# Seven-product MLP: input tiles in pairs, the first chunk as a pipeline over pairs, GpSimd out of the cross output stage, six weight blocks ahead

## The chip, the core and the metric

The kernel runs on one core of one Trainium2 chip. The metric is the device time of one execution in microseconds (us), as a median over runs. TensorE is called PE here, VectorE DVE, ScalarE ACT, GpSimd POOL and SyncE SP, as the profile calls them.

## The reference

A decoder trunk of two layers, 512 tokens, model width 1024, all in float32. In each layer

```
h = h + W_out [ MLA(n) | DiffAttn(n) | MoBA(n) ],  n = RMSNorm(h)
h = h + CrossAttn(RMSNorm(h), RMSNorm(mem))
h = h + W2 relu(W1 RMSNorm(h))^2
```

and the trunk ends with a final RMSNorm. The change touches two places of a layer: the output projection of the cross attention (a 1024 x 1024 matrix, `w_co`), and the MLP behind it (`w1` 1024 x 4096, `w2` 4096 x 1024).

## The kernel before

**Number format.** Every operand of a matmul is held as two halves, a rounded part ("hi") and the rest ("lo"), side by side in one tile. A product is three matmuls: hi with hi, hi with lo, lo with hi (`mm3`). So every weight block that arrives by DMA costs one ACT cast (hi, L157 or L266) and one subtraction on DVE or POOL (lo, L162 or L267), and so does every activation tile (`split`, L140 and L142).

**The cross output stage** (`output` with `halves`, L1058). For m = 0 to 7 in this order, 24 matmuls of 128x512 (8 input tiles, 3 matmuls each) give 128 rows of the projection; DVE adds them to the residual tile `h[m]` (L1056); `half_input` (L1072) then makes the inputs of the MLP from it. For m < 4 that is the block called 11 and the difference t1. For m >= 4 it is 21, 22, and, with the scaled tile y that was kept from m - 4, the combinations t2, t3 and t4. Squares of h are summed over m (L409 on ACT, L412 on POOL, the last on DVE) for the norm. The w_co blocks are halved on DVE and POOL in turn (L162).

**The MLP** works in four chunks c of 1024 hidden columns, each in four pairs g = 0 to 3, called a to d below (two blocks of 128 hidden columns each). A pair is computed with seven products instead of eight, Strassen's way: product n takes one combination of the four quarter blocks of w1 (11, 12, 21, 22, or the sums s1 to s4) and one combination of the inputs:

```
FACTORS = {1: ("11", "11"), 2: ("12", "21"), 3: ("s4", "22"), 4: ("22", "t4"), 5: ("s1", "t1"), 6: ("s2", "t2"), 7: ("s3", "t3")}
```

A product is 4 input tiles x 3 matmuls = 12 matmuls of 128x256. "1a" is product 1 of pair a of the first chunk. Products 1 and 5 need only the inputs of m < 4; 2, 3, 4, 6 and 7 need those of m >= 4 too. `combination` (L242) fetches the quarter blocks, forms a sum on DVE (L263), casts on ACT (L266) and subtracts on DVE (L267); L1291, L1293, L1295 and L1300 (ACT) and L1288 and L1296 (DVE) collect the products from PSUM, and `evict` (L1308 to L1311) applies the squared ReLU. The products of a chunk are followed by the "down" blocks with w2, which run beside the products of the next chunk.

**What sets the order.** `planned` lists all weight blocks in the order of use, `mlp_order` those of the MLP. `weights` keeps `look` blocks ahead of the one in use: 2 until the MLP begins, then `mlp_look` = 6. In the MLP `vector_all` keeps the subtractions on DVE. All weight loads are issued by SP, in order. Tiles rotate through a few places each: `raw` has 4, `w` 5, `tmp` 11; of PSUM banks `mm` has 3 and `s` has 3. The order within each engine's queue is then fixed when the program is built; each engine works its queue in that order.

Of the kernel before, what the change touches and what calls it, by code (L numbers as in the profile page):

```python
# [17 lines left out]
KT = 8  # L18
# [83 lines left out]
class Trunk:  # L102
# [62 lines left out]
    def planned(self):  # L165

        a = self.a

        def halves(t):
            return [t[:, :S], t[:, S:]]  # L170

        for l in range(L):
            names = {"kv": [0], "cq": [1, 2], "d0": [3, 4], "d1": [5, 6]}
            names.update({n: [7 + 3 * j, 8 + 3 * j, 9 + 3 * j] for j, n in enumerate(("d2", "o0", "o1"))})
            for n in self.fill_order.split():
                for j in names.get(n, ()):
                    yield from halves(a["w_in"][l, j])
                if n == "tok":
                    for k in range(KT):
                        yield a["w_v"][l, k]  # L180
                if n[0] == "m" and n != "mem":
                    yield from (a["w_mla"][l, int(n[1]), :, :4 * P], a["w_mla"][l, int(n[1]), :, 4 * P:])
                if n == "cross":
                    for m in range(KT):
                        yield from halves(a["w_ck"][l, m])
                    for j in range(2 * KT):
                        yield a["w_cv"][l, j]
            for w in (a["w_out"][l], a["w_cq"][l], a["w_co"][l]):
                for m in range(KT):
                    yield from halves(w[m])  # L190
            for kind, c, m in self.mlp_order(l):
                if kind == "down":
                    yield from halves(a["w2"][l, c, m])
                else:
                    yield l, c, m, self.FACTORS[kind][0]
# [14 lines left out]
        return w  # L210

    FACTORS = {1: ("11", "11"), 2: ("12", "21"), 3: ("s4", "22"), 4: ("22", "t4"), 5: ("s1", "t1"), 6: ("s2", "t2"),
               7: ("s3", "t3")}

    @staticmethod
    def mlp_order(l):


        late = []
        for g in range(KT // 2):
            parts = [4, 3] if late else [None, None]
            for n, then in zip((1, 5, 2, 6, 7), (None, None, None, *parts)):
                yield n, 0, g
                if then:
                    yield then, 0, late[0]
            late = [g]
        for n in (4, 3):
            yield n, 0, late[0]  # L230
        for c in range(4):
            for g in range(KT // 2):
                if c < 3:
                    for n in (1, 5, 6, 2, 7):
                        yield n, c + 1, g
                yield "down", c, 2 * g
                if c < 3:
                    for n in (4, 3):
                        yield n, c + 1, g
                yield "down", c, 2 * g + 1  # L240

    def combination(self, l, c, g, name):  # L242

        nc = self.nc
        got = self.quads.setdefault((l, c, g), {})

        def block(n):
            if n not in got:
                src = self.a["w1"][l, c * KT + 2 * g + int(n[0]) - 1]
                t = self.sb.tile([P, S], F32, tag=tags[n], name=self.name("raw"), bufs=self.bufs[tags[n]])  # L250
                at = (int(n[1]) - 1) * S
                nc.sync.dma_start(t, src[:, at:at + S])
                got[n] = t
            return got[n]

        tags = {"11": "raw", "21": "raw", "12": "tmp", "22": "tmp"}
        sums = {"s1": ("21", "22", ALU.add), "s2": ("s1", "11", ALU.subtract), "s3": ("11", "21", ALU.subtract),
                "s4": ("12", "s2", ALU.subtract)}
        if name in sums:
            x, y, op = sums[name]  # L260
            x, y = (got[n] if n in sums else block(n) for n in (x, y))
            got[name] = self.tmp()
            nc.vector.tensor_tensor(got[name], x, y, op)  # L263
        raw = got[name] if name in sums else block(name)
        w = self.pair("w" if name in ("12", "22", "s4") else "B")
        nc.scalar.copy(w[:, 0, :], raw)  # L266
        nc.vector.tensor_tensor(w[:, 1, :], raw, w[:, 0, :].bitcast(F32), ALU.subtract)  # L267
        return w
# [789 lines left out]
    def output(self, w, outs, gain, order=range(KT), halves=None):  # L1058

        self.sum_squares_start()  # L1060
        hn = []
        for m in range(KT):
            ps = self.proj(w[m], lambda k: (outs[k][:, 0, :], outs[k][:, 1, :]), S, order)
            self.add_to_h(m, ps)
            if halves is None:
                hn.append(self.norm_input(m, gain))
            else:
                self.half_input(m, gain, halves)
        self.hn = hn
        self.hnorm = self.norm(self.sq, NQ, 2)  # L1070

    def half_input(self, k, gain, parts):  # L1072


        nc = self.nc
        n = S // 2
        j = k % 4
        y = self.tmp()
        nc.scalar.activation(y, self.h[k], AF.Copy, scale=gain[:, k:k + 1])  # L1079
        p = self.pair("A")  # L1080
        if k < KT // 2:
            self.split(p[:, 0, :n], p[:, 1, :n], y[:, :n])
            nc.vector.tensor_tensor(y[:, :n], y[:, n:], y[:, :n], ALU.subtract)
            self.split(p[:, 0, n:], p[:, 1, n:], y[:, :n])
            parts["11"].append(p[:, :, :n])
            parts["t1"].append(p[:, :, n:])

            parts["y"].append(y)
        else:
            self.split(p[:, 0, :], p[:, 1, :], y)  # L1090
            parts["21"].append(p[:, :, :n])
            parts["22"].append(p[:, :, n:])
            if j == 0:
                a, b, c = self.prob_tile(), self.prob_tile(), self.pair("B")
                parts["t23"] = [t[:, :, i * S:(i + 1) * S] for t in (a, b) for i in range(2)]
                parts["room"] = a[:, :, 2 * S:], b[:, :, 2 * S:], c[:, :, :n], c[:, :, n:]
            two, one = parts["t23"][j], parts["room"][j]
            t = self.tmp()
            nc.vector.tensor_tensor(t.rearrange("p (a c) -> p a c", c=n),
                                    y[:, n:].unsqueeze(1).to_broadcast([P, 2, n]),  # L1100
                                    parts["y"][j].rearrange("p (a c) -> p a c", c=n), ALU.subtract)
            nc.vector.tensor_tensor(y[:, :n], y[:, :n], t[:, :n], ALU.subtract)  # L1102
            self.split(two[:, 0, :], two[:, 1, :], t)
            self.split(one[:, 0, :], one[:, 1, :], y[:, :n])
            parts["t2"].append(two[:, :, :n])
            parts["t3"].append(two[:, :, n:])
            parts["t4"].append(one)
        self.sum_squares_add(self.h[k], k == KT - 1)

    def memory_norm(self, ticks, step):  # L1110

# [278 lines left out]
    def run(self):  # L1390
# [25 lines left out]
        g = self.gains  # L1416
# [11 lines left out]
        for l in range(L):  # L1428
            gs = slice(l * KT, (l + 1) * KT)
            self.vector_full = True  # L1430
            outs = self.mixer(l)
            self.vector_full = False
            self.output(self.a["w_out"][l], outs, g["g_cross"][:, gs], (3, 0, 4, 1, 5, 2, 6, 7))
            outs = self.cross(l)
            parts = {n: [] for n in ("11", "21", "22", "t1", "t2", "t3", "t4", "y")}
            self.output(self.a["w_co"][l], outs, g["g_mlp"][:, gs], halves=parts)
            self.vector_all, self.look = True, self.mlp_look
            self.mlp(l, g["g_attn"][:, (l + 1) * KT:(l + 2) * KT] if l + 1 < L else None, parts)
            self.vector_all, self.look = False, 2

# [100 lines left out]
```

## Time and profile before

| | |
|---|---|
| median of 3 runs | 1551.61 us (1550.52 to 1551.83) |
| the profiled execution | 1549.21 us, span 1547.4 us |
| PE busy | 1487.4 us, 96% of the span, 8648 matmuls |
| DVE busy | 1081.7 us, 70% |
| ACT busy | 854.6 us, 55% |
| POOL busy | 414.6 us, 27% |
| cross output stage and first MLP chunk, first layer | 389 to 492 us |
| the same, second layer | 1144 to 1246 us |

The two stages of the change come once in each layer. The span is that of the profiled execution, and its time is 2.40 us below the median of the unprofiled runs. Shares of the whole span say little here, since the stages have different limits; the rows below are of the two stages.

### The profile page before, as it was taken

To read this page: it belongs to the slowest core of one execution; us is meant where nothing else is said; L and a number is where in the kernel's file an instruction comes from. 1 tells how busy PE (TensorE), PEld (TensorE's weight loads), DVE (VectorE), ACT (ScalarE), POOL (GpSimd) and SP (SyncE) were. 2 spreads that over 40 slices of the span, in tenths; PEclk is the share of its full clock that TensorE was granted. 3 is DMA by queue.
4 is the path that set the end of the run, shared out by engine and by line. 5 is a ranking of instruction groups with operands and counts; after the bars stand their busy time and mean duration, and the time that the engine had idled before them with its cause. 6 is when DMAs were issued, how large, how long until landed. Compare 5 with 4: busy or idle time off the path is not lost.

```text
span 1547.4 us, 24601 instructions
## 1 busy us (share of the span) xinstructions
PE 1487.4 (96%) x8648; PEld 1299.8 (84%) x8648; DVE 1081.7 (70%) x2391; ACT 854.6 (55%) x1884; POOL 414.6 (27%) x336
## 2 busy tenths in 40 slices
PE   7799999999989999999998999999998999999997
PEld 5678797888879989988887878888887998998886
DVE  7688888535689667675437898883378986677653
ACT  5566778535456445454436667764355654454441
POOL 5645365342310000000136445644512000000001
PEclk9999999999999999999999999999999999999998
DMA  4444454221223332332324535423302333323321
GB/s 141 123 112 127 124 151 122 80 97 49 75 78 115 96 103 92 106 110 89 96 75 107 148 100 151 132 83 102 101 29 69 103 110 102 102 96 110 109 96 55
DMA packets 90141, 157.25 MB, mean 102 GB/s; under 512 B 12065, under 2 KB 17057, under 8 KB 90017
## 3 DMA queue, kind: packets, MB, share of 16 engines
q1 hardware_dynamic: 89728, 155.63, 32.6%
q8 instruction: 68, 1.11, 0.3%
q14 instruction: 57, 0.46, 0.1%
q10 hardware_dynamic: 288, 0.05, 0.0%
HBM read 136.24 MB, written 2.10 MB: 89 GB/s over the span
## 4 chain that ended last, share of the span: by engine, by line
PE 76%; DVE 14%; ACT 4%; issue 3%; POOL 1%; DMA 1%; SPq 0%; POOLq 0%; DVEq 0%; ACTq 0%
PE mm L279 60%; PE s L279 12%; PE t L282 3%; DVE tmp L635 2%; DVE B L142 1%; DVE tmp L700 1%; ACT tmp L637 1%; DVE pt L660 1%; DVE A L142 1%; PE t L279 1%; POOL w L162 1%; ACT tmp L1079 1%; DVE small L977 1%; DVE tmp L1102 1%; ACT B L140 1%
## 5 line engine op out<-in xcount | busy, mean ns | idle before, releaser
L279 PE MATMUL mm<-B,w 128*128 128x512 f32 (+1 forms) x2490 | 571.3, 386 | 3.9 <-DVE B L145 2.2
L279 PEld LDWEIGHTS mm<-B,w 128*128 128x128 f32 x2490 | 451.8, 188 | 98.5 <-DVE tmp L881 3.0
L279 PE MATMUL mm<-A,w 128*128 128x512 f32 (+1 forms) x1920 | 389.5, 353 | 16.8 <-ACT A L144 5.8
L279 PEld LDWEIGHTS mm<-A,w 128*128 128x128 f32 x1920 | 313.3, 192 | 63.7 <-DVE A L145 5.9
L157 ACT CAST w<-raw 128x512 fp32r<-128x512 f32 (+1 forms) x372 | 225.1, 607 | 256.2 <-PE mm L279 187.2
L162 POOL TENSOR_TENSOR w<-raw,w 128x512 fp32r<-128x512 f32 (+2 forms) x199 | 255.3, 1292 | 275.0 <-ACT w L157 248.6
L412 POOL TENSOR_TENSOR tmp<-tmp,tmp 128x512 f32<-128x512 f32 (+1 forms) x37 | 46.5, 1257 | 693.5 <-ACT tmp L409 672.6
L162 DVE TENSOR_TENSOR w<-raw,w 128x512 fp32r<-128x512 f32 x173 | 122.1, 706 | 27.0 <-ACT w L157 26.8
L637 ACT ACTIVATE tmp<-tmp,small 128x384 f32<-128x384 f32 (+3 forms) x176 | 99.1, 563 | 71.1 <-DVE small L635 65.8
L1056 DVE TENSOR_TENSOR h<-mm,h 128x512 f32<-128x512 f32 x92 | 63.2, 687 | 69.4 <-PE mm L279 69.3
L279 PE MATMUL mm<-pt,B 128*128 128x256 f32 x768 | 102.8, 283 | 0.3 <-ACT tmp L1293 0.3
L140 ACT CAST B<-tmp 128x512 fp32r<-128x512 f32 (+2 forms) x156 | 91.6, 591 | 19.3 <-DVE tmp L779 4.4
L266 ACT CAST B<-tmp 128x512 fp32r<-128x512 f32 x96 | 59.6, 621 | 69.3 <-DVE tmp L263 69.0
L279 PEld LDWEIGHTS mm<-pt,B 128*128 128x128 f32 x768 | 96.5, 191 | 0.8 <-ACT tmp L1293 0.5
L263 DVE TENSOR_TENSOR tmp<-raw,raw 128x512 f32<-128x512 f32 x64 | 44.0, 687 | 65.0 <-DMA raw<-w 65.0
L142 DVE TENSOR_TENSOR B<-tmp,B 128x512 fp32r<-128x512 f32 (+1 forms) x110 | 81.4, 740 | 11.1 <-ACT B L140 8.3
L282 PE MATMUL t<-ident,tmp 128*128 128x128 f32 (+1 forms) x444 | 73.9, 273 | 8.5 <-DVE tmp L825 4.6
L142 POOL TENSOR_TENSOR B<-tmp,B 128x512 fp32r<-128x512 f32 (+1 forms) x46 | 62.5, 1366 | 44.5 <-ACT B L140 39.3
L282 PEld LDWEIGHTS t<-ident,tmp 128*128 128x128 f32 (+1 forms) x444 | 54.3, 140 | 22.9 <-DVE tmp L825 5.4
L660 DVE TENSOR_TENSOR pt<-t,pt 128x256 fp32r<-128x256 f32 (+1 forms) x192 | 66.9, 370 | 7.0 <-ACT pt L657 6.0
L279 PE MATMUL s<-pt,B 128*128 128x512 f32 (+3 forms) x352 | 71.0, 345 | 0.0
L657 ACT CAST pt<-t 128x256 fp32r<-128x256 f32 (+1 forms) x192 | 58.0, 333 | 16.3 <-PE t L282 15.6
(194 smaller groups left out, 2137.3 us busy)
## 6 DMA issues: line engine op xcount, KB each, us to landing
raw<-w SPq DMA_DIRECT2D x256, 256.0 KB, 2.8
raw<-w_in SPq DMA_DIRECT2D x64, 256.0 KB, 3.2
st<-B SPq DMA_DIRECT2D x144, 64.0 KB, 2.0
raw<-w_ck SPq DMA_DIRECT2D x32, 256.0 KB, 3.0
raw<-w_cv SPq DMA_DIRECT2D x32, 256.0 KB, 2.6
raw<-w_out SPq DMA_DIRECT2D x32, 256.0 KB, 2.8
raw<-w_cq SPq DMA_DIRECT2D x32, 256.0 KB, 2.6
raw<-w_co SPq DMA_DIRECT2D x32, 256.0 KB, 2.6
```

Of the source, the lines that this page charges most:

```text
L140: nc.scalar.copy(hi, x)
L142: eng.tensor_tensor(lo, x, hi.bitcast(F32), ALU.subtract)
L157: self.nc.scalar.copy(w[:, 0, :], raw)
L162: eng.tensor_tensor(w[:, 1, :], raw, w[:, 0, :].bitcast(F32), ALU.subtract)
L266: nc.scalar.copy(w[:, 0, :], raw)
L279: self.in_order(self.nc.tensor.matmul(out, lhs, rhs, start=start, stop=stop, skip_group_check=open), hold)
L282: self.in_order(self.nc.tensor.transpose(out, x, self.ident))
L412: eng.tensor_tensor(s[:, :n], s[:, :n], self.sq[:, :n], ALU.add)
L637: nc.scalar.activation(t[:, :n], t[:, :n], AF.Exp, bias=st[:, 0:1], scale=-1.0, accum_out=st[:, 1:2])
L657: nc.scalar.copy(hi, src)
L660: nc.vector.tensor_tensor(lo, src, hi.bitcast(F32), ALU.subtract)
L1056: nc.vector.tensor_tensor(self.h[m], ps, self.h[m], ALU.add)
```

## The change

Five edits, made for both layers:

1. The cross output stage goes through m in the order 0, 4, 1, 5, 2, 6, 3, 7 (`BY_PAIRS`), in the plan of the weights and in the loop.
2. `vector_all` is set before that stage, not after it: POOL no longer halves w_co blocks there, and the squares are summed on DVE (`sum_squares_add(..., True)`).
3. `look` becomes 6 at the seventh block of the stage (m = 3), not at the start of the MLP.
4. The first chunk's products follow a written list that mixes the pairs, 1a 5a 1b 5b first; the last two (4d, 3d) go in behind the first products of the second chunk.
5. The block "12" of the first chunk takes a `raw` place instead of a `tmp` one.

```diff
--- before.py
+++ after.py
@@ -185,9 +185,9 @@
                         yield from halves(a["w_ck"][l, m])
                     for j in range(2 * KT):
                         yield a["w_cv"][l, j]
-            for w in (a["w_out"][l], a["w_cq"][l], a["w_co"][l]):
-                for m in range(KT):
-                    yield from halves(w[m])
+            for n in ("w_out", "w_cq", "w_co"):
+                for m in range(KT) if n != "w_co" else self.BY_PAIRS:
+                    yield from halves(a[n][l, m])
             for kind, c, m in self.mlp_order(l):
                 if kind == "down":
                     yield from halves(a["w2"][l, c, m])
@@ -210,6 +210,9 @@
         return w
 
 
+    BY_PAIRS = 0, 4, 1, 5, 2, 6, 3, 7
+
+
 
     FACTORS = {1: ("11", "11"), 2: ("12", "21"), 3: ("s4", "22"), 4: ("22", "t4"), 5: ("s1", "t1"), 6: ("s2", "t2"),
                7: ("s3", "t3")}
@@ -218,21 +221,16 @@
     def mlp_order(l):
 
 
-        late = []
-        for g in range(KT // 2):
-            parts = [4, 3] if late else [None, None]
-            for n, then in zip((1, 5, 2, 6, 7), (None, None, None, *parts)):
-                yield n, 0, g
-                if then:
-                    yield then, 0, late[0]
-            late = [g]
-        for n in (4, 3):
-            yield n, 0, late[0]
+        for step in "1a 5a 1b 5b 2a 6a 2b 7a 6b 4a 3a 7b 1c 4b 5c 3b 2c 6c 1d 7c 5d 4c 2d 6d 3c 7d".split():
+            yield int(step[0]), 0, "abcd".index(step[1])
+        late = [(4, 0, 3), (3, 0, 3)]
         for c in range(4):
             for g in range(KT // 2):
                 if c < 3:
                     for n in (1, 5, 6, 2, 7):
                         yield n, c + 1, g
+                        if late:
+                            yield late.pop(0)
                 yield "down", c, 2 * g
                 if c < 3:
                     for n in (4, 3):
@@ -253,7 +251,7 @@
                 got[n] = t
             return got[n]
 
-        tags = {"11": "raw", "21": "raw", "12": "tmp", "22": "tmp"}
+        tags = {"11": "raw", "21": "raw", "12": "tmp" if c else "raw", "22": "tmp"}
         sums = {"s1": ("21", "22", ALU.add), "s2": ("s1", "11", ALU.subtract), "s3": ("11", "21", ALU.subtract),
                 "s4": ("12", "s2", ALU.subtract)}
         if name in sums:
@@ -1059,7 +1057,9 @@
 
         self.sum_squares_start()
         hn = []
-        for m in range(KT):
+        for i, m in enumerate(range(KT) if halves is None else self.BY_PAIRS):
+            if halves is not None and i == 6:
+                self.look = self.mlp_look
             ps = self.proj(w[m], lambda k: (outs[k][:, 0, :], outs[k][:, 1, :]), S, order)
             self.add_to_h(m, ps)
             if halves is None:
@@ -1105,7 +1105,7 @@
             parts["t2"].append(two[:, :, :n])
             parts["t3"].append(two[:, :, n:])
             parts["t4"].append(one)
-        self.sum_squares_add(self.h[k], k == KT - 1)
+        self.sum_squares_add(self.h[k], True)
 
     def memory_norm(self, ticks, step):
 
@@ -1433,8 +1433,8 @@
             self.output(self.a["w_out"][l], outs, g["g_cross"][:, gs], (3, 0, 4, 1, 5, 2, 6, 7))
             outs = self.cross(l)
             parts = {n: [] for n in ("11", "21", "22", "t1", "t2", "t3", "t4", "y")}
+            self.vector_all = True
             self.output(self.a["w_co"][l], outs, g["g_mlp"][:, gs], halves=parts)
-            self.vector_all, self.look = True, self.mlp_look
             self.mlp(l, g["g_attn"][:, (l + 1) * KT:(l + 2) * KT] if l + 1 < L else None, parts)
             self.vector_all, self.look = False, 2
```

What this does to the queues is shown at three places, in the first layer. The second layer's queues change in the same way.

PE at the start of the MLP. `mm_1131` is the bank of the last w_co block; A tiles are 11 and t1 (1075, 1083, 1091, 1099) or 21 and 22 (the others), pt tiles t2 and t3, B and w the weights. Before, the end of 1a, then 5a, 2a, the start of 1b, 6a:

```order
L279 MATMUL mm_1144_5059<-A_1099_4837,B_1133_5005 128x256 x3
L279 MATMUL s_1157_5102<-A_1075_4697,B_1137_5026 128x256 x3
L279 MATMUL s_1157_5102<-A_1083_4743,B_1137_5026 128x256 x3
L279 MATMUL s_1157_5102<-A_1091_4790,B_1137_5026 128x256 x3
L279 MATMUL s_1157_5102<-A_1099_4837,B_1137_5026 128x256 x3
L279 MATMUL mm_1160_5120<-A_1107_4884,w_1146_5062 128x256 x3
L279 MATMUL mm_1160_5120<-A_1119_4938,w_1146_5062 128x256 x3
L279 MATMUL mm_1160_5120<-A_1128_4989,w_1146_5062 128x256 x3
L279 MATMUL mm_1160_5120<-A_1139_5044,w_1146_5062 128x256 x3
L279 MATMUL mm_1173_5190<-A_1075_4697,B_1152_5077 128x256 x3
L279 MATMUL mm_1173_5190<-A_1083_4743,B_1152_5077 128x256 x2
L279 MATMUL mm_1144_5059<-pt_1108_4887,B_1148_5067 128x256 x6
```

Now, the end of 5a, then 1b, 5b, the column sums of the squares, 6a (A_1141 is the input of m = 3, the last of the four 11 and t1 tiles):

```order
L277 MATMUL s_1157_5102<-A_1141_5021,B_1133_4977 128x256 x3
L277 MATMUL mm_1162_5122<-A_1075_4697,B_1135_4982 128x256 x3
L277 MATMUL mm_1162_5122<-A_1095_4797,B_1135_4982 128x256 x3
L277 MATMUL mm_1162_5122<-A_1112_4895,B_1135_4982 128x256 x3
L277 MATMUL mm_1162_5122<-A_1141_5021,B_1135_4982 128x256 x3
L277 MATMUL s_1165_5141<-A_1075_4697,B_1139_5003 128x256 x3
L277 MATMUL s_1165_5141<-A_1095_4797,B_1139_5003 128x256 x3
L277 MATMUL s_1165_5141<-A_1112_4895,B_1139_5003 128x256 x3
L277 MATMUL s_1165_5141<-A_1141_5021,B_1139_5003 128x256 x3
L277 MATMUL t_1167_5157<-ones2_93,tmp_1151_5078 128x2 x4
L277 MATMUL mm_1154_5083<-pt_1084_4746,B_1147_5050 128x256 x6
L277 MATMUL mm_1154_5083<-pt_1085_4747,B_1147_5050 128x256 x6
```

Four products that need only the tiles of m < 4 now stand behind the last w_co block, where two stood; 2a has moved behind 6a.

DVE around the eviction of the last w_co block (`h7`). L1099, L1102 and L142 are `half_input`, L263 and L267 the sums and the lo halves of w1 blocks. Before:

```order
L267 TENSOR_TENSOR B_1133_5005<-raw_1132_5003,B_1133_5005 128x512
L263 TENSOR_TENSOR tmp_1136_5024<-raw_1134_5020,raw_1135_5022 128x512
L1056 TENSOR_TENSOR h7_84<-mm_1131_5002,h7_84 128x512
L267 TENSOR_TENSOR B_1137_5026<-tmp_1136_5024,B_1137_5026 128x512
L1099 TENSOR_TENSOR tmp_1140_5047<-tmp_1138_5042,tmp_1098_4835 128x512
L263 TENSOR_TENSOR tmp_1147_5065<-tmp_1136_5024,raw_1132_5003 128x512
L142 TENSOR_TENSOR A_1139_5044<-tmp_1138_5042,A_1139_5044 128x512
L142 TENSOR_TENSOR pt_1109_4888<-tmp_1140_5047,pt_1109_4888 128x512
L1102 TENSOR_TENSOR tmp_1138_5042<-tmp_1138_5042,tmp_1140_5047 128x256
L412 TENSOR_TENSOR tmp_1141_5054<-tmp_1141_5054,tmp_1130_4999 128x512
L142 TENSOR_TENSOR B_1110_4889<-tmp_1138_5042,B_1110_4889 128x256
L267 TENSOR_TENSOR B_1148_5067<-tmp_1147_5065,B_1148_5067 128x512
```

Now, up to the same eviction, behind the sum s1a (L261 and L265 are L263 and L267 of before, L410 is L412, L1054 is L1056):

```order
L265 TENSOR_TENSOR B_1129_4968<-raw_1128_4966,B_1129_4968 128x512
L1054 TENSOR_TENSOR h3_76<-mm_1123_4955,h3_76 128x512
L265 TENSOR_TENSOR B_1133_4977<-tmp_1132_4975,B_1133_4977 128x512
L265 TENSOR_TENSOR B_1135_4982<-raw_1134_4980,B_1135_4982 128x512
L261 TENSOR_TENSOR tmp_1138_5001<-raw_1136_4997,raw_1137_4999 128x512
L261 TENSOR_TENSOR tmp_1146_5048<-tmp_1132_4975,raw_1128_4966 128x512
L410 TENSOR_TENSOR tmp_1142_5027<-tmp_1142_5027,tmp_1122_4952 128x512
L265 TENSOR_TENSOR B_1139_5003<-tmp_1138_5001,B_1139_5003 128x512
L142 TENSOR_TENSOR A_1141_5021<-tmp_1140_5019,A_1141_5021 128x256
L265 TENSOR_TENSOR B_1147_5050<-tmp_1146_5048,B_1147_5050 128x512
L1083 TENSOR_TENSOR tmp_1140_5019<-tmp_1140_5019 128x256
L1054 TENSOR_TENSOR h7_84<-mm_1143_5030,h7_84 128x512
```

Eight sums and lo halves of w1 blocks, enough for 1a, 5a, 1b, 5b and 6a, have moved ahead of the eviction of `h7`, where two stood.

SP, the loads of the first chunk. `raw` in a name is that of the fetched block, whatever place it takes. Before, in order 11a, 21a, 11b, 21b, 22a, 12a, 22b, 11c:

```order
L252 DMA raw_1132_5003<-w1 128x512
L252 DMA raw_1134_5020<-w1 128x512
L252 DMA raw_1151_5075<-w1 128x512
L252 DMA raw_1153_5080<-w1 128x512
L252 DMA raw_1135_5022<-w1 128x512
L252 DMA raw_1145_5060<-w1 128x512
L252 DMA raw_1154_5082<-w1 128x512
L252 DMA raw_1177_5210<-w1 128x512
```

Now 11a, 21a, 11b, 21b, 22a, 22b, 12a, 12b:

```order
L250 DMA raw_1128_4966<-w1 128x512
L250 DMA raw_1130_4971<-w1 128x512
L250 DMA raw_1134_4980<-w1 128x512
L250 DMA raw_1136_4997<-w1 128x512
L250 DMA raw_1131_4973<-w1 128x512
L250 DMA raw_1137_4999<-w1 128x512
L250 DMA raw_1144_5031<-w1 128x512
L250 DMA raw_1155_5084<-w1 128x512
```

12a now takes the place of 11a and 12b that of 21a among the four `raw` places, so both loads wait until DVE has formed s3a from 11a and 21a, and everything behind them on SP waits too.

## Rows read from the trace of the kernel before

**Rows 1.** Windows, first layer: PE, PEld, DVE, ACT, POOL busy (count), PEclk, DMA, GB/s.

```profile
394.40:433.00 38.60, 38.60 (x169) 31.38 (x168) 29.85 (x37) 21.46 (x40) 14.21 (x11) 1.00 0.25 83
433.00:448.00 15.00, 9.97 (x54) 8.97 (x54) 13.35 (x23) 8.02 (x15) 0.53 (x1) 0.77 0.25 87
448.00:491.80 43.80, 42.63 (x358) 42.07 (x357) 39.99 (x74) 30.42 (x63) 1.40 (x1) 1.00 0.28 91
491.80:740.00 248.20, 248.20 (x1546) 222.80 (x1545) 167.69 (x284) 119.24 (x224) 0.00 (x0) 1.00 0.32 102
```

**Rows 2.** The same windows of the second layer, behind its cross output stage.

```profile
1188.60:1203.60 15.00, 10.88 (x60) 10.20 (x59) 13.33 (x23) 8.37 (x17) 0.51 (x1) 0.77 0.25 85
1203.60:1246.20 42.60, 41.77 (x352) 41.44 (x352) 39.97 (x74) 30.14 (x63) 1.40 (x1) 1.00 0.29 93
```

**Rows 3.** Timeline of PE, first layer: start, length, matmuls, idle before and its releaser.

```profile
395.60 37.47 PE L279 MATMUL mm<-B,w 128*128 128x512 f32 x163
...
434.82 0.51 PE L279 MATMUL mm<-A,B 128*128 128x256 f32 x2 [1.75 <-ACT B L266]
...
441.39 0.80 PE L279 MATMUL mm<-A,w 128*128 128x256 f32 x2 [2.43 <-ACT w L266]
...
448.01 0.95 PE L279 MATMUL t<-ones,tmp 128*128 128x2 f32 x8
448.82 0.96 PE L279 MATMUL mm<-A,B 128*128 128x256 f32 x6
...
453.53 0.62 PE L282 MATMUL t<-ident,rcol 128*128 128x128 f32 x4 [0.84 <-DVE rcol L347]
453.91 1.68 PE L279 MATMUL mm<-A,w 128*128 128x256 f32 x12
...
459.65 1.58 PE L279 MATMUL s<-A,w 128*128 128x256 f32 x12
...
473.81 1.60 PE L279 MATMUL mm<-A,w 128*128 128x256 f32 x12
...
491.77 5.66 PE L279 MATMUL mm<-B,w 128*128 128x512 f32 x24
```

**Rows 4.** Timeline of PE, second layer: last w_co matmuls, first down block.

```profile
1186.65 1.99 PE L279 MATMUL mm<-B,w 128*128 128x512 f32 x8
...
1246.17 5.20 PE L279 MATMUL mm<-B,w 128*128 128x512 f32 x22
```

**Rows 5.** DVE groups by form, 394 to 433 us: count, busy us, mean ns, idle before.

```profile
L142 DVE TENSOR_TENSOR A<-tmp,A 128x256 fp32r<-128x256 f32 x8 | 7.2, 900 | 5.8 <-ACT A L140 5.8
L1083 DVE TENSOR_TENSOR tmp<-tmp 128x256 f32<-128x256 f32 x4 | 4.6, 1139 | 0.2
L1102 DVE TENSOR_TENSOR tmp<-tmp,tmp 128x256 f32<-128x256 f32 x3 | 4.4, 1473 | 0.1
```

**Rows 6.** Timeline of DVE, three instructions back to back.

```profile
445.03 0.69 DVE L263 TENSOR_TENSOR tmp<-raw,raw 128x512 f32<-128x512 f32 x1
445.63 0.42 DVE L1288 TENSOR_TENSOR tmp<-mm,tmp 128x256 f32<-128x256 f32 x1
445.96 0.68 DVE L263 TENSOR_TENSOR tmp<-tmp,raw 128x512 f32<-128x512 f32 x1
```

**Rows 7.** Timeline of DVE and POOL at one moment of the cross output stage.

```profile
420.75 1.30 POOL L412 TENSOR_TENSOR tmp<-tmp,tmp 128x512 f32<-128x512 f32 x1 [3.87 <-ACT tmp L409]
420.83 1.50 DVE L1102 TENSOR_TENSOR tmp<-tmp,tmp 128x256 f32<-128x256 f32 x1
```

**Rows 8.** Timeline of ACT and POOL: half input, cast, and the power for the norm.

```profile
436.80 0.72 ACT L1079 ACTIVATE tmp<-h,gains 128x512 f32<-128x512 f32 x1
437.55 0.62 ACT L140 CAST A<-tmp 128x512 fp32r<-128x512 f32 x1
...
449.24 1.40 POOL L341 TENSOR_TENSOR small<-small,mhalf 128x4 f32<-128x4 f32 x1 [15.71 <-DVE small L375]
```

**Rows 9.** Loads of line 252, 405 to 500 us, from issue to landing.

```profile
DMA to landing us min/median/max: 2.5/3.0/4.8
```

## The prediction, as it was made before the changed kernel ran

> **What bounds the kernel now.** I read the windows by stage first, then PE's timeline in the stretch that they point to, then DVE's groups there. In the cross output stage PE is busy 38.60 of 38.60 us, and in the later chunks of the MLP 248.20 of 248.20, both at granted clock 1.00: nothing that DVE, ACT, POOL or a load does there costs anything as long as PE is fed. Between them PE is busy only 9.97 of 15.00 us at a mean clock of 0.77 (a mix of the two levels, 2.4 and 1.2 GHz), then 42.63 of 43.80, while DVE is busy 13.35 of 15.00 and 39.99 of 43.80 [rows 1]. The second layer shows the same [rows 2]. So the loss sits at the start of the MLP, and DVE is the engine waited for.
>
> How large is it? The last w_co matmul ends at 395.60 + 37.47 = 433.07, the first down block starts at 491.77 [rows 3]: 58.70 us. In between PE has the 28 products of chunk 1 and five of chunk 2, 33 in all. Ten products in steady flow go from 459.65 to 473.81, 1.416 each [rows 3], so 33 are 46.73; the column sums take 0.81 (448.01 to 448.82) and the broadcast 0.38 (453.53 to 453.91). That is 47.92 of work, so 10.8 us are lost. In the second layer 1188.64 to 1246.17 is 57.53 [rows 4], 9.6 lost. Together **20.4 us**, which is the most that this change can win. In the first layer idle time is 5.0 + 1.2 = 6.2 of the 10.8 [rows 1]; the rest is matmuls at the lower clock behind the gaps, and their ramps. The gaps are 1.75 us before 1a and 2.43 before 2a, both for a cast that itself waited for DVE [rows 3].
>
> **The change part by part.** T is the end of the last w_co matmul. A w_co block is 24 of the 163 matmuls, 5.52 us [rows 3].
>
> *DVE load of the output stage.* In steady flow DVE spends 0.60 us on a 512-wide and 0.33 on a 256-wide instruction, start to start (445.03, 445.63, 445.96) [rows 6]. POOL's work moves to it: 13 instructions per layer (7 lo halves, 6 sums of squares), 12 of them inside the stage: +7.2 us. But the 256-wide ones there take 900, 1139 and 1473 ns on average instead of 420 [rows 5, 6], and the one at 420.83 ends with a POOL instruction that started 0.08 us earlier plus about its own 0.3 [rows 7]. I take the excess as POOL's doing: 8 x 0.48 + 4 x 0.72 + 3 x 1.05 = 9.9 us. DVE's 29.85 us become 29.85 - 9.9 + 7.2 = 27.1 of 38.6 [rows 1], and the eight w1 instructions that now come ahead of the last eviction (4.8) make 31.9. It fits. If the excess had another cause, it would be 41.9, 3.3 too much; that is the upper bound of this cost, the lower is a gain of latency.
>
> By a rule of the Trainium skill the move points the wrong way: "Perfetto Trace Analysis", section Optimizing Scalar/DVE Operations, says that with DVE saturated it may make sense to offload work to ScalarE or even GpSimd, and adds that between DVE and GpSimd it might not help, as they share an SBUF read port. By its first half the sum is the 41.9 above, by its second, and by the row, the 31.9. The moment shown in [rows 7] sides with the second half.
>
> *The start of the MLP.* I walk the queues with these steps, an eviction 0.25 after its block. Block m = 6 ends at T - 11.0: eviction, y on ACT (0.72 [rows 8]), then DVE's seven instructions, done by T - 6.2; s1a and 11a lo by T - 5.0; eviction of m = 3 (it ended at T - 5.5) by T - 4.4; then s1a lo, 11b lo, s1b, s2a, the squares, s1b lo, half of the input of m = 3, s2a lo, at T + 0.1. So 1a starts at T without a gap, and 5a, 1b, 5b follow: 4 x 1.416 carry PE to T + 5.7, the column sums to T + 6.5. The last 11 and t1 tile, wanted by 5a at T + 2.5, is there at T + 1.4. Under this cover DVE makes the tiles of m = 7: eviction T + 1.1, y on ACT, t3 and the rest to T + 5.0. So 6a runs from T + 6.5. Before, with two products as cover and this same work ahead, 2a started at T + 8.3 [rows 3].
>
> *What is late next.* 12a and 12b wait for a raw place until s3a is formed (T + 5.6). They land 3.0 us after issue (2.5 to 4.8 [rows 9]), at T + 8.6; cast 0.62 [rows 8], s4a, s3b, lo half: 2a can run from T + 10.4. Two thirds of 6b and 7a stand ahead of the bulk of it and last to T + 10.6. The power for the norm (1.40 on POOL [rows 8]) falls under the same cover. Behind 2a come three matmuls of 4a, and then 2b, which needs the PSUM bank of 2a: there are three mm banks, and DVE gets to that eviction at about T + 12.6, PE at T + 12.5. I charge 0.4 us for this knot. The SP queue behind it (11c, 21c, 12c) is wanted only at T + 18 and later, and lands by T + 14.
>
> *The middle of the chunk.* From the eviction of m = 7 to the lo half of s4d, the last weight of chunk 1, DVE has 36.8 us of instructions (54 of 512, 12 of 256, 4 tiny); PE, without a gap, wants it at T + 42.4. So 5.1 us may go in waits; at 5d it is tightest, 2.5. My walk has 1.3 us of waits up to s4a and 1 to 2 more for 12b, 21d and 12d: DVE stays just ahead, and I charge 1.1 us. So each layer still loses about 1.5 us (bounds 0.3 and 8, below), where it lost 10.8 and 9.6: **-17.4 us**. Edits 1, 3 and 4 are one thing here: without the pairs t2 of m = 3 and 7 would not be alone at the end, without the earlier look the weights of 1b and 5b would not be there. Edit 5 costs nothing while 6a, 6b and 7a cover the load; without that cover it costs up to 4.8 + 0.6. Nothing behind gives the gain back, since PE is gapless there before [rows 1].
>
> The profiled execution took 1549.21 us, so 1531.8 in its terms; it was 2.4 below the median of the runs, 1551.61, so the prediction is **1534.2 us**.
>
> **The rivals.** *DVE paces the chunk.* Its waits do not shrink: it idles 1.65 + 3.81 = 5.5 us in the two windows now [rows 1]; less the 2.5 of slack at 5d that is 3.0 of new stall, plus 0.5 at the knot: 3.5 per layer, gain 13.4, 1538. With both ring loads at 4.8 instead of 3.0, another 3.6: 7.1 per layer, gain 6.2, 1545. For it: DVE's work between T and the first down block hardly shrinks. Against: those waits were for PE, POOL and casts that stood idle with it.
>
> *DVE overfull in the output stage.* If the excess of [rows 5] is not POOL's, DVE has 41.9 us of work in 38.6 and enters the MLP 3.3 us late in each layer: gain 17.4 - 6.6 = 10.8, 1541. For it speaks only that the excess is inferred; against it stands the moment of [rows 7]. This is what the first half of the rule of the Trainium skill ("Perfetto Trace Analysis", above) would make of the change.
>
> *Loads behind the raw ring.* This one makes it slower. SP works in order and DVE too: if each of five turns of the four places in a chunk (12a, 11c, 12c, 11d, 21d) leaves DVE standing for a landing and a cast (4.8 + 0.6), that is 27 us per layer; less the slack of 5, PE loses 22 and the kernel becomes about 24 us slower, 1575. It decides from about 12 us of exposed waits in a chunk, more than two whole turns beyond the slack. Against it: between the instruction that frees a place and the one that needs the new block DVE has three to seven others, 2 to 4 us, about as long as a landing.
>
> *No change.* The early products move forward, but the chunk still ends with DVE's last weight at the old time: within 3 us of 1551.6. It needs 8 us more of DVE waits per layer than I count; DVE idled 5.5 in all.
>
> **How the numbers follow.** Forecast 62% (1532 to 1537), DVE paces 21% (1537 to 1546), DVE overfull 4% (1541), better than the bound of 20.4 by a shift elsewhere 2%, no change 6%, slower 5%. From 1531.0 (all of the 20.4) to 1544.0 lie the forecast and most of the next two cases: 8 in 10. Faster by over 0.2% (about 3 us, what a measurement can tell from no change): 89%; within: 6%; slower: 5%.
>
> **What would show it.** PE's timeline: no gap between the last w_co matmul and 1a, granted clock near 1.00 in the 15 us behind it, 6a about 6.5 us after it; first down block some 49 to 50 us after it instead of 58.7 and 57.5. DVE: no 256-wide instruction over 0.5 us in the output stage, about 27 to 32 us busy there. SP: 12a issued some 5.6 us after the last w_co matmul, landing about 3 us later. Wrong would be: w_co matmuls that wait for an eviction or a weight (DVE overloaded), a wait of PE for w or of DVE for raw of over 2 us (the ring), or waits for DVE spread over 5c to 7d (the first rival).

## The result and the profile after

The changed kernel takes **1535.78 us** (median of 4 runs, 1534.85 to 1538.51), the kernel before in the same session 1551.72; the ratio is 0.9899, with a 95% interval of 0.9881 to 0.9916: about 16 us less. The profiled execution took 1538.51 us (span 1536.7) and was the slowest of the four.

Windows of the changed kernel, in the columns of [rows 1]: the cross output stage, the 15 us behind its last matmul (at T = 434.81) and the rest up to the first down block; then the last two of the second layer (T = 1183.31).

```profile
395.90:434.80 38.90, 38.90 (x172) 31.91 (x172) 31.25 (x56) 24.50 (x45) 0.00 (x0) 1.00 0.26 88
434.80:449.80 15.00, 14.77 (x125) 14.56 (x124) 13.57 (x29) 9.82 (x20) 1.38 (x1) 1.00 0.33 106
449.80:484.90 35.10, 34.19 (x287) 33.70 (x286) 33.94 (x62) 25.53 (x52) 0.00 (x0) 1.00 0.32 104
...
1183.30:1198.30 15.00, 14.77 (x125) 14.56 (x124) 13.62 (x29) 9.82 (x20) 1.39 (x1) 1.00 0.33 106
1198.30:1235.10 36.80, 34.25 (x287) 33.65 (x286) 34.43 (x63) 25.45 (x52) 0.00 (x0) 1.00 0.30 99
```

PE is busy 14.77 of the 15 us, where it was 9.97, and its mean clock there is 1.00, where it was 0.77 [rows 1]. DVE's load in the output stage went from 29.85 to 31.25 us, with 19 instructions more. What is left of PE's idle time lies later: 0.9 us in the third window, 2.55 in the last.

Timeline of PE, both layers, in the columns of [rows 3]: last w_co matmul, 1a, column sums, 6a and the start of 6b, first down block; then the second layer.

```profile
390.70 44.11 PE L277 MATMUL mm<-B,w 128*128 128x512 f32 x192
434.64 1.58 PE L277 MATMUL mm<-A,B 128*128 128x256 f32 x12
...
440.30 0.95 PE L277 MATMUL t<-ones,tmp 128*128 128x2 f32 x8
441.11 1.92 PE L277 MATMUL mm<-pt,B 128*128 128x256 f32 x14
...
484.87 5.66 PE L277 MATMUL mm<-B,w 128*128 128x512 f32 x24
...
1139.20 44.11 PE L277 MATMUL mm<-B,w 128*128 128x512 f32 x192
...
1213.53 1.70 PE L277 MATMUL mm<-pt,B 128*128 128x256 f32 x12 [1.43 <-ACT tmp L1293]
...
1233.56 1.69 PE L277 MATMUL mm<-pt,B 128*128 128x256 f32 x12 [0.76 <-ACT tmp L1293]
1235.09 5.66 PE L277 MATMUL mm<-B,w 128*128 128x512 f32 x24
```

1a starts without a gap (1.75 us in [rows 3]), 6a 6.3 us after T. From T to the first down block it is now 484.87 - 434.81 = 50.06 us and 51.78 in the second layer, where it was 58.70 and 57.5. Of work there are 47.92 in it, so 2.1 and 3.9 us are still lost, 6.0 in all, where it was 20.4: **14.4 us gained in these two places**. The two profiled executions themselves differ by 10.7 us only (1549.21 and 1538.51): outside these places that of the changed kernel is 3.7 us longer, 1.74 of it ahead of the first cross output stage (which takes PE 44.11 us in both), where only the order of the first w_co loads differs. Over the kernels below T of the first layer lies between 432.71 and 436.38, so a single execution tells little outside the two places, and the loss is counted from T.

For the experiments the loss is counted in the same way, up to the second down block, since some kernels put a product inside the first: in both kernels it starts 8.29 us after the first (491.77 and 500.06 before), so loss = (second down block - T) - 56.21.

### The profile page after: what moved, and what is told of

Its sections match the earlier page's. It is cut to its first block, busy times and chain, and to the rows that moved or that the text cites. A ratio compares the mean times of both kernels' runs of the same rounds, so it can differ in the third digit from the quotient of the medians.

```text
span 1536.7 us, 24586 instructions
## 1 busy us (share of the span) xinstructions
PE 1486.8 (97%) x8648; PEld 1299.4 (85%) x8648; DVE 1075.2 (70%) x2417; ACT 855.3 (56%) x1884; POOL 378.9 (25%) x310
## 4 chain that ended last, share of the span: by engine, by line
PE 79%; DVE 11%; ACT 4%; issue 3%; DMA 2%; POOL 1%; SPq 0%; POOLq 0%; DVEq 0%; ACTq 0%
PE mm L277 63%; PE s L277 12%; PE t L280 3%; DVE tmp L633 2%; DMA raw<-w 1%; DVE B L142 1%; DVE pt L658 1%; ACT tmp L635 1%; DVE tmp L698 1%; PE t L277 1%; POOL w L162 1%; ACT B L140 1%; DVE small L975 1%; DVE tmp L261 1%; DVE tmp L695 0%
## 5 line engine op out<-in xcount | busy, mean ns | idle before, releaser
L162 POOL TENSOR_TENSOR w<-raw,w 128x512 fp32r<-128x512 f32 (+1 forms) x185 | 235.6, 1283 | 214.9 <-ACT w L157 195.0
L410 POOL TENSOR_TENSOR tmp<-tmp,tmp 128x512 f32<-128x512 f32 (+1 forms) x25 | 30.9, 1234 | 656.4 <-ACT tmp L407 654.3
L162 DVE TENSOR_TENSOR w<-raw,w 128x512 fp32r<-128x512 f32 x187 | 131.7, 704 | 34.9 <-ACT w L157 34.7
L1054 DVE TENSOR_TENSOR h<-mm,h 128x512 f32<-128x512 f32 x92 | 63.2, 687 | 69.8 <-PE mm L277 69.5
L261 DVE TENSOR_TENSOR tmp<-raw,raw 128x512 f32<-128x512 f32 x64 | 44.0, 688 | 67.7 <-DMA raw<-w 67.7
L142 DVE TENSOR_TENSOR B<-tmp,B 128x512 fp32r<-128x512 f32 (+1 forms) x110 | 81.8, 743 | 13.2 <-ACT B L140 9.8
L142 POOL TENSOR_TENSOR B<-tmp,B 128x512 fp32r<-128x512 f32 (+1 forms) x46 | 62.4, 1364 | 48.9 <-ACT B L140 43.6
L339 POOL TENSOR_TENSOR small<-small,mhalf 128x4 f32<-128x4 f32 (+2 forms) x19 | 23.7, 1245 | 202.8 <-DVE small L373 172.4
```

The lines of the kernel that those rows point to most:

```text
L142: eng.tensor_tensor(lo, x, hi.bitcast(F32), ALU.subtract)
L162: eng.tensor_tensor(w[:, 1, :], raw, w[:, 0, :].bitcast(F32), ALU.subtract)
L410: eng.tensor_tensor(s[:, :n], s[:, :n], self.sq[:, :n], ALU.add)
L1054: nc.vector.tensor_tensor(self.h[m], ps, self.h[m], ALU.add)
```

## The experiments

All are shown in one table; "loss" is that of both layers, from each one's PE timeline, and the ratio is to the kernel before on the same chip (whose median there was 1550.35 to 1551.72, so medians of different rows compare to about 1 us).

| kernel | edits in it | median us | ratio, 95% interval | loss us |
|---|---|---|---|---|
| before | none | 1551.61 | 1 | 10.8 + 9.6 = 20.4 |
| pool_out_only | 2 | 1549.28 | 0.9985 [0.9975, 0.9995] | 8.1 + 9.5 = 17.6 |
| pool_look | 2, 3 | 1535.77 | 0.9905 [0.9890, 0.9919] | 4.5 + 2.5 = 7.0 |
| tmp12_rows | 2, 3, 4 | 1533.45 | 0.9887 [0.9868, 0.9905] | 1.3 + 0.6 = 2.0 |
| b_tmp12 | 1, 2, 3, 4 | 1531.68 | 0.9883 [0.9869, 0.9896] | 1.2 + 1.1 = 2.2 |
| the change | 1 to 5 | 1535.78 | 0.9899 [0.9881, 0.9916] | 2.1 + 3.9 = 6.0 |
| after_again | 1 to 5 | 1536.75 | 0.9908 [0.9893, 0.9923] | 2.0 + 3.4 = 5.3 |
| pool_back | 1, 3, 4, 5 | 1544.28 | 0.9959 [0.9947, 0.9971] | 6.4 + 7.1 = 13.5 |
| squares_back | 1, half of 2, 3, 4, 5 | 1540.57 | 0.9939 [0.9925, 0.9953] | 3.5 + 5.0 = 8.4 |
| look_late | 1, 2, 4, 5 | 1545.49 | 0.9970 [0.9959, 0.9981] | 7.8 + 5.4 = 13.2 |
| old_list | 1, 2, 3, 5 | 1537.78 | 0.9920 [0.9907, 0.9933] | 3.6 + 4.1 = 7.7 |
| row_order | 2, 3, 4, 5 | 1534.93 | 0.9903 [0.9890, 0.9916] | 1.1 + 2.7 = 3.8 |
| raw5 | 1 to 5, five raw places | 1533.49 | 0.9893 [0.9879, 0.9906] | 0.7 + 1.3 = 2.0 |
| pool_noise | 1 to 5, POOL busy for nothing | 1536.91 | 0.9914 [0.9899, 0.9928] | 2.1 + 3.9 = 5.9 |

20.4 less the loss, and the time that the ratio gives, agree within about 2.5 us in every row (before minus look_late: 7.2 and 4.7; minus tmp12_rows: 18.4 and 17.5), so within that what the edits do, they do in these two places. A loss is that of one execution each.

**POOL back** (edit 2 undone).

```diff
+            self.output(self.a["w_co"][l], outs, g["g_mlp"][:, gs], halves=parts)
             self.vector_all = True
-            self.output(self.a["w_co"][l], outs, g["g_mlp"][:, gs], halves=parts)
...
-        self.sum_squares_add(self.h[k], True)
+        self.sum_squares_add(self.h[k], k == KT - 1)
```

> The changed kernel with edit 2 undone: POOL again takes every second lo half of the w_co blocks and the sums of squares in the cross output stage. Theory (POOL's work slows DVE's 256-wide instructions): they take 0.9 to 1.5 us again instead of 0.42, DVE is busy about 31.25 - 7.2 + 9.9 = 34 us in the stage, some of it late for the first weights, so PE waits 1 to 2 us more per layer: 1538 to 1540 us. Rival (the stretched instructions had another cause, and DVE's load decides): DVE busy 24 us there, 1535 us or less.

The mechanism is as the theory has it, its price larger: 13.5 us are lost instead of 6.0, 1544.28 us. DVE's groups by form in the output stage, first of the changed kernel, then of this one:

```profile
L142 DVE TENSOR_TENSOR A<-tmp,A 128x256 fp32r<-128x256 f32 x7 | 2.9, 419 | 0.9 <-ACT A L140 0.9
...
L1083 DVE TENSOR_TENSOR tmp<-tmp 128x256 f32<-128x256 f32 x3 | 1.3, 425 | 0.1
L1102 DVE TENSOR_TENSOR tmp<-tmp,tmp 128x256 f32<-128x256 f32 x3 | 1.3, 419 | 0.0
```

```profile
L142 DVE TENSOR_TENSOR A<-tmp,A 128x256 fp32r<-128x256 f32 x6 | 5.4, 904 | 4.4 <-ACT A L140 4.4
...
L1102 DVE TENSOR_TENSOR tmp<-tmp,tmp 128x256 f32<-128x256 f32 x3 | 4.4, 1453 | 0.2
...
L1083 DVE TENSOR_TENSOR tmp<-tmp 128x256 f32<-128x256 f32 x3 | 3.2, 1076 | 0.1
```

With POOL there, DVE starts 40 instructions in the stage instead of 56 and is busy as long: 31.99 us against 31.25. Not only the 256-wide ones are stretched: the 512-wide lo halves of t2 and t3 (L142, pt) take 1416 ns on average instead of 685. By the end of the stage DVE is late: its eviction of m = 3 starts 1.88 us before T (432.58), where it was 5.13 (429.68). How it reaches PE: a sum of squares on POOL lies across the sum s2a, and that holds the last input of 1a. Timelines of DVE, POOL and PE in this kernel:

```profile
435.16 1.78 DVE L261 TENSOR_TENSOR tmp<-tmp,raw 128x512 f32<-128x512 f32 x1
436.86 0.68 DVE L265 TENSOR_TENSOR B<-tmp,B 128x512 fp32r<-128x512 f32 x1
437.46 0.41 DVE L142 TENSOR_TENSOR A<-tmp,A 128x256 fp32r<-128x256 f32 x1
```

```profile
435.12 1.27 POOL L410 TENSOR_TENSOR tmp<-tmp,tmp 128x512 f32<-128x512 f32 x1 [5.03 <-ACT tmp L407]
```

```profile
436.25 0.39 PE L277 MATMUL mm<-A,B 128*128 128x256 f32 x1 [0.73 <-ACT A L140]
437.93 0.51 PE L277 MATMUL mm<-A,B 128*128 128x256 f32 x2 [1.28 <-DVE A L142]
```

The sum takes 1.78 instead of 0.68 us, 1a stands 0.73 and 1.28 us, the mean clock of the 15 us behind T falls to 0.89, and the column sums come 9.5 us after T instead of 5.5.

**Only the squares back on POOL**, the lo halves stay on DVE (the second half of the diff above).

> The changed kernel with only the sums of squares back on POOL (six per layer), the lo halves stay on DVE. Theory (any POOL instruction of this kind slows DVE's 256-wide instructions beside it): DVE's 256-wide mean rises from 0.42 to between 0.6 and 1.0 us, time between the changed kernel and the one with all of POOL's work back, 1536 to 1538 us. Rival (DVE's load decides): 3.6 us less of DVE work, 1534 to 1536 us, 0.42 us stays.

The theory's sign, again more than expected: 1540.57 us. The 256-wide L142 take 742 ns on average and the three L1102 1420. Each POOL instruction holds one DVE instruction, here in the timelines of both:

```profile
409.15 1.30 POOL L410 TENSOR_TENSOR tmp<-tmp,tmp 128x512 f32<-128x512 f32 x1 [3.84 <-ACT tmp L407]
```

```profile
409.35 1.39 DVE L142 TENSOR_TENSOR A<-tmp,A 128x256 fp32r<-128x256 f32 x1 [1.01 <-ACT A L140]
```

POOL ends at 410.45, DVE 0.29 later. The rival falls: taking six instructions from DVE made the kernel slower. In the trace 2.4 us of the 4.8 between the medians (of two sessions) are found; its profiled execution (1538.28) was the fastest of five, and where the others lose the rest stays open.

**POOL busy for nothing.** The changed kernel with a product on POOL that nobody reads:

```diff
             self.add_to_h(m, ps)
+            if halves is not None:
+                noise = self.sb.tile([P, S], F32, tag="noise", name=self.name("noise"), bufs=1)
+                self.nc.gpsimd.tensor_tensor(noise, self.h[m], self.h[m], ALU.mult)
```

> The changed kernel, and for each m of the cross output stage POOL squares h[m] into a tile that nobody reads: 16 POOL instructions more, nothing taken from DVE, nobody waits for their result. Theory (DVE stands still while a POOL instruction runs): the 256-wide DVE instructions go to 0.7 to 1.4 us on average, DVE is busy 36 to 38.9 us in the stage, and the kernel loses as much as with the squares on POOL or more: 1540 to 1547 us. Rival (POOL's cost was its own lateness on the chain of squares and lo halves): 1534 to 1537 us and 0.42 us.

The theory in this form missed, and both of the rival's numbers were met: 1536.91 us, as the changed kernel beside it (1536.75), and 0.42 us for the 256-wide ones. DVE was busy 32.06 us in the 38.90 up to T (396.40 to 435.30), 0.81 more than in the changed kernel; POOL was busy 12.17 us there, of which 4.08 belong to an instruction that waited for DVE. The rival's reason does not hold for the two kernels above, though: with POOL back PE is busy 38.90 of 38.90 us in the stage, so no lo half came too late for it, and in squares_back POOL's last sum ends at 433.68, while DVE comes to the instruction that needs it at 438.81. POOL's timeline here and DVE's (L1102 is L1099 of the change):

```profile
403.23 1.41 POOL L1067 TENSOR_TENSOR noise<-h 128x512 f32<-128x512 f32 x1 [4.04 <-DVE h L1054]
...
431.22 6.82 POOL L1067 TENSOR_TENSOR noise<-h 128x512 f32<-128x512 f32 x2 [4.97 <-DVE h L1054]
```

```profile
403.05 0.69 DVE L162 TENSOR_TENSOR w<-raw,w 128x512 fp32r<-128x512 f32 x1
403.94 1.25 DVE L1102 TENSOR_TENSOR tmp<-tmp,tmp 128x512 f32<-128x512 f32 x1 [0.20 <-ACT tmp L1082]
...
437.35 1.24 DVE L1102 TENSOR_TENSOR tmp<-tmp,tmp 128x512 f32<-128x512 f32 x1 [0.21 <-ACT tmp L1082]
```

A DVE instruction that becomes ready while POOL runs is held to POOL's end and takes its own time from there (403.23 + 1.41 = 404.64, DVE ends at 405.19, 0.55 later). The other way round POOL waits: from 429.19 to 437.15 DVE goes from one instruction to the next, and of the two POOL instructions in the 6.82 us the first takes 5.64. It is the longest of all 16:

```profile
L1067 POOL TENSOR_TENSOR noise<-h x16: 1042/1384/5641, 397.7 to 1186.1; 128x512 f32<-128x512 f32 x16
```

Eight DVE instructions that began later went ahead of it, each begun before the one in front had ended. It ended at 436.86, 0.98 us after DVE began the eviction of `h7` (435.88), which reads one of its inputs from PSUM; whether that let it in is not tested. This noise starts right behind an eviction, when DVE has work at hand, so in the stage it holds only the three L1099 noticeably (1168 ns on average instead of 693). The squares start behind ACT's square, and each of the six in squares_back starts 0.03 to 0.22 us before the DVE instruction that it holds. That this is why the squares cost time and the noise does not is read off these rows; no run moves the noise to the place of the squares. That the two engines hold each other is what the Trainium skill, "SBUF — State Buffer", section Who interferes with whom, states: a DVE instruction with two SBUF inputs and a GpSimd instruction that reads SBUF exclude each other, and the one that issues first holds the port for its whole length. The trace agrees in both directions, with the numbers above.

**POOL out alone** (the kernel before with edit 2), and **POOL out with the early look** (edits 2 and 3).

> The kernel before with edit 2 alone: POOL out of the cross output stage. Theory (POOL slows DVE there): DVE's 256-wide instructions fall to 0.42 us, DVE has about 27 us of work of 38.6, the gap before 1a goes, that before 2a stays: 2 to 5 us faster than before, 1547 to 1550 us. Rival (without the list DVE only waits more): within 1 us of 1551.7. Rival (DVE overfull): 4 to 7 us slower.

1549.28 us; by the ratio 2.3 us of gain, at the lower end of the theory's. The runs go from 1544.00 to 1550.76, and the medians differ by 1.07 us only, so the time alone hardly parts the theory from the first rival; the trace does, with DVE busy 28.19 us in the 38.90 of the stage. The second rival falls. The gap before 1a is gone but for 0.27 us, that before 2a is as it was: here windows and PE.

```profile
434.30:449.30 15.00, 11.55 (x78) 10.35 (x77) 11.61 (x23) 8.45 (x16) 1.39 (x1) 0.89 0.22 72
```

```profile
440.04 0.51 PE L279 MATMUL mm<-A,w 128*128 128x256 f32 x2 [2.41 <-ACT w L266]
```

The edit that pool_look has beside edit 2 (`BY_PAIRS` is 0 to 7 in order there):

```diff
-        for m in range(KT):
+        for i, m in enumerate(range(KT) if halves is None else self.BY_PAIRS):
+            if halves is not None and i == 6:
+                self.look = self.mlp_look
...
-            self.vector_all, self.look = True, self.mlp_look
```

> The kernel before with edits 2 and 3 alone: POOL out, early look; old list, old order of m, block 12 in tmp. Theory (edits 2 and 3 together give DVE the lead, and the list adds some 3 us): 1535 to 1540 us. Rival (as the prediction has it, pairs, look and list are one thing, and without the list 2a stands for m = 7 and 12a): 1544 to 1549 us.

1535.77 us, the theory's; the rival, which was the prediction's own words, falls. With the old list:

```profile
435.10:450.10 15.00, 13.04 (x103) 12.11 (x102) 13.82 (x30) 8.75 (x18) 1.38 (x1) 1.00 0.31 101
```

```profile
437.71 1.24 PE L282 MATMUL mm<-A,w 128*128 128x256 f32 x9
440.13 0.38 PE L282 MATMUL mm<-A,w 128*128 128x256 f32 x1 [1.18 <-ACT A L140]
```

2a stands third, as before, but it has its weight, does the 9 matmuls of m = 4 to 6 and waits 1.18 us for m = 7. The clock stays at 1.00.

**The early look undone.**

```diff
-            if halves is not None and i == 6:
-                self.look = self.mlp_look
...
             self.output(self.a["w_co"][l], outs, g["g_mlp"][:, gs], halves=parts)
+            self.look = self.mlp_look
```

> The changed kernel with edit 3 undone: six weight blocks ahead only from the start of the MLP. Theory: the weights of 1b and 5b then stand behind DVE's work for m = 7, PE has a gap of about 3 us behind 5a and the clock falls there: 7 to 11 us slower than the changed kernel, 1543 to 1547 us. Rival (the list of products alone carries the gain): within 2 us of 1535.8.

As the theory has it, 1545.49 us. 5b waits for its weight's cast 2.21 us, and the mean clock falls to 0.77:

```profile
433.60:448.60 15.00, 12.63 (x78) 12.03 (x77) 12.66 (x24) 9.58 (x19) 1.39 (x1) 0.77 0.13 42
```

```profile
439.98 0.50 PE L277 MATMUL s<-A,B 128*128 128x256 f32 x2 [2.21 <-ACT B L264]
```

**The old list** (edit 4 undone: 1a 5a 2a 6a 7a 1b ...) and **the old order of m** (edit 1 undone: `BY_PAIRS = 0, 1, 2, 3, 4, 5, 6, 7`).

> The changed kernel with the old list of products (edit 4 undone; pairs, POOL out, early look and the raw place of 12 stay). Theory: 2a stands third again and needs the tiles of m = 7 and 12a, which are there about 7 to 8 us behind the last w_co block; PE stands 4 to 5 us per layer, plus the lower clock: 1544 to 1549 us. Rival (what counts is that DVE enters the MLP with less work behind it): 1536 to 1539 us.

The rival's range: 1537.78 us, with an interval that overlaps that of the changed kernel. 2a waits 0.34 us for m = 7, no more; that it would stand for it and for 12a was wrong.

> The changed kernel with edit 1 undone: the cross output stage goes through m = 0 to 7 again, with the written list of products. Theory: the four blocks with the heavier work (m = 4 to 7, about 3.7 us of DVE each, and 1.2 for the w_co halves, of 5.5 us of PE) then stand together with eight instructions of w1 (4.8 us) among them, so DVE is about 2.5 us late for 6a and what follows: 2 to 6 us slower, 1538 to 1542 us. Rival (four products of cover are enough in any order of m): within 1 us of 1535.8.

The rival's again: 1534.93 us. The pairs gain nothing that these runs can tell: 6a starts 6.30 us after T here too, and the loss is 3.8, less than with them (6.0, or 5.3 in after_again).

**The raw places.** What is left of the loss: from T to the first down block PE's listed waits, 1.2 us in the first layer and 2.8 in the second, are all for copies on ACT. ACT's timeline of the changed kernel, first layer, then second; then, for the second, the sum s3c on DVE and the two loads that wait for it on SP.

```profile
460.84 0.62 ACT L264 CAST w<-raw 128x512 fp32r<-128x512 f32 x1 [1.94 <-DMA raw<-w]
...
1210.88 0.62 ACT L264 CAST w<-raw 128x512 fp32r<-128x512 f32 x1 [3.48 <-DMA raw<-w]
...
1213.11 0.36 ACT L1293 COPY tmp<-mm 128x256 f32<-128x256 f32 x1
```

```profile
1204.98 0.68 DVE L261 TENSOR_TENSOR tmp<-raw,raw 128x512 f32<-128x512 f32 x1
```

```profile
L250 SPq DMA_DIRECT2D raw<-w x2: 328/380/431, 1205.7 to 1206.1; - x2
...
DMA to landing us min/median/max: 4.5/4.6/4.8
```

The cast is that of 12d. Its load needs the place of 21c, which is free when DVE has formed s3c, at 1205.66; SP issued it at 1206.1, and it landed 4.8 us later. ACT works in order, so the copy L1293 that reads 6c's result, before 7c may add to the same bank, comes at 1213.11, and 7c waits for it on PE the 1.43 us shown above. DVE's own longest wait for a load in these stretches is 0.97 us (for 21d, just ahead of 12d). In the first layer the wait of 1.94 us did not reach 7c: the same copy ends at 463.43, and PE comes to 7c at 463.49 without a wait.

> The changed kernel with five raw places instead of four. Theory (what is left of the loss is ACT, which works in order, standing at a cast for a load that waited for a raw place): the waits of ACT for raw of 1.94 and 3.48 us and the waits of PE for the copy behind them (1.43 and 0.8) go, so 2.1 + 3.9 us of loss become about 1 to 1.5 each: 3 us faster than the changed kernel, 1532 to 1534 us. Rival (DVE paces the chunk): the load is earlier, PE's waits stay or move, within 1 us of 1535.8.

With `"raw": 5` the theory's loss and range: 2.0 us instead of 6.0 (or 5.3), 1533.49 us; no wait of ACT for raw is left in the chunk of the first layer, and 0.7 us in that of the second. The interval of the ratio overlaps that of the changed kernel; the waits decide, not the time.

> The changed kernel with edit 5 undone: block 12 of the first chunk in a tmp place again. Theory (the raw ring is what holds the loads up): 12a to 12d no longer wait for the sums s3 but for a tmp place, which is free earlier or later as the eleven turn; if the raw ring is the cause, ACT's waits for raw shrink and the kernel is 0 to 3 us faster, 1533 to 1536 us. Rival (tmp is the tighter ring, since products and sums live there long): loads wait for evictions, 2 to 8 us slower, 1538 to 1544 us.

With `"12": "tmp"` (edit 5 undone) 1531.68 us, a little better than the theory's range, and a loss of 2.2. The intervals of the ratio overlap here too; but all four runs (1531.12 to 1532.49) lie below all eight of the changed kernel in its two sessions (1534.57 to 1538.51), though the two were not run side by side. The rival, that tmp is the tighter ring, falls. The first layer's two windows show what is left:

```profile
433.70:448.70 15.00, 15.00 (x126) 14.77 (x126) 13.71 (x30) 9.92 (x20) 1.39 (x1) 1.00 0.28 91
448.70:483.60 34.90, 34.47 (x288) 33.98 (x287) 33.33 (x60) 25.09 (x51) 0.00 (x0) 1.00 0.30 103
```

**A smaller change**: edits 2, 3 and 4 alone, and the changed kernel once more beside it.

> The changed kernel with edits 1 and 5 undone: m = 0 to 7 in order, block 12 of the first chunk in a tmp place; edits 2, 3 and 4 stay. Theory (the gain comes from POOL's absence, the early look and the list; the pairs and the raw place bring nothing, and the raw place costs 3 to 4 us by ACT standing for a load): 1530 to 1534 us, faster than the changed kernel. Rival (each alone is harmless, but without the pairs the tmp places are too few for the loads of 12): 1536 us or more.

> The changed kernel once more, as the measure for the others beside it: 1533 to 1537 us, 14.5 to 16.5 us under the kernel before.

1533.45 and 1536.75 us. The trace has 2.0 us of loss against 5.3, which is the difference; the two intervals of the ratio still overlap by 0.0012. That of b_tmp12, from another session, has the lowest median of all. Both have a lower median and less loss than the changed kernel, and neither is clear of it by its interval: the pairs can go, and by the traces the raw place of 12 should.

## Why the prediction was right, and where not

1534.2 us was forecast and 1535.78 measured, with the sign and the place as argued, and the start of the MLP as walked. Three other steps did not hold. That the time came within 1.6 us although the loss was 3.0 above its forecast is no merit: the four runs lie 3.7 us apart. The bound for "all of the 20.4" is 1531.2, not 1531.0, which changes nothing.

- *No gap before 1a, four products as cover.* Right to a few tenths: 6a at T + 6.3 (6.5 forecast), s3a formed at T + 5.6 (DVE's sum at 439.77, 0.69 long, ends at 440.46; forecast T + 5.6), the clock at 1.00, first down block 50.06 us after T in the first layer (49 to 50), but 51.78 in the second.
- *DVE's load in the output stage.* 31.25 us measured, 31.9 forecast; no 256-wide instruction over 0.43 us. That the excess of [rows 5] was POOL's doing is shown by pool_back and squares_back; the rival "DVE overfull" falls. pool_noise adds what the prediction did not have: POOL work in the stage need not cost time, and the rows point to the moment at which it starts.
- *"Edit 5 costs nothing while 6a, 6b and 7a cover the load."* This step failed. It holds for 12a (2a starts at T + 9.9, 10.4 forecast). But 12b to 12d go through the same four places, and 12d was late in both layers; undoing the edit takes 3.8 us of loss away (1.8 where the pairs are undone too). That is more than the whole error of the sum: 3.0 us of loss were forecast in the two layers (1.5 each), 6.0 measured.
- *"DVE stays just ahead, and I charge 1.1 us."* The size was too small, and the wait was put on the wrong engine. I walked the loads against DVE's order, and DVE indeed never waits more than 1 us for a load; it is ACT, in order, whose copies stand behind a cast that waits for a load (1.43 us of PE behind one of them).
- *"Edits 1, 3 and 4 are one thing here."* Wrong, as pool_look and row_order show. Added one after another, in the trace: edit 2 takes 2.8 us of loss away, edit 3 another 10.6, edit 4 another 5.0, edit 1 nothing (2.0 and 2.2 are left), and edit 5 gives 3.8 back. Edit 2 is worth 2.8 alone and 7.5 as the last one in, edit 4 only 1.7 as the last one. By their intervals the times part for edits 2 and 3; for 4 and 5 they overlap, and the traces alone speak. Edit 3 without edit 2 was not run.
- *The rivals.* "DVE paces the chunk" was right that a loss of some 3 us a layer could remain (3.5 each there), wrong in the reason: with five raw places 0.7 and 1.3 remain, and DVE has the same work. "Loads behind the raw ring" named the resource, with 22 us of PE a layer; it cost 1.9.

## What to carry to other kernels

Before one moves work between stages, see what a stage's first products wait for: here, with POOL out, more than half of the gain came with two lines that prepare weights two blocks earlier, and of the reordering that looked like the core the pairs gave nothing and the list less. Walk a late load through every engine that works in order behind it: its victim was a copy on ACT that had nothing to do with the load. A small instruction on a second engine can cost more than it takes off the first; look for instructions whose length has two values in one trace, and see what ran beside the long ones.

## What was not expected of the hardware

POOL and DVE wait for each other in both directions: a 0.42 us DVE instruction took 1.39 behind a POOL instruction of 1.30, and a POOL instruction that takes 1.04 to 1.52 us elsewhere in that stage took 5.64 beside a DVE that went on without a gap. And eight POOL instructions in the output stage of a layer (pool_noise) cost nothing measurable, where six (squares_back, 7.77 us of POOL) that each started just ahead of a DVE instruction cost 2.4 us in the trace and 4.8 between the medians. That the moment of the start makes the difference is not shown by a run of its own.
